# Seven block products on all 16 K tiles for a head's in-projection, chained from raw weight tiles

## The chip, the cores and the metric

One core of one Trainium2 chip. The metric is the device time of one execution of the whole program in microseconds (us); lower is better. The program is one launch with all weights in device memory.

## The reference

Two residual layers on one sequence of T = 512 tokens with D = 2048 channels, all in float32. The first is a gated differential attention layer, the second an RWKV-7 layer. Cut to what the change touches:

```python
def diff_attention_mixer(h, ...):            # h: (1, 512, 2048), RMS-normed x
    proj = h @ w_in                          # 2048 x 8192: q, k, v, gate
    q, k, v, gate = jnp.split(proj, 4, axis=-1)
    q = apply_rope(rms_norm(q.reshape(B, T, 8, 2, 128), q_gain), cos, sin)
    k = apply_rope(rms_norm(k.reshape(B, T, 8, 2, 128), k_gain), cos, sin)
    v = v.reshape(B, T, 8, 256)
    o = causal_diff_attention(q, k, v, lam)  # softmax(q0 k0) - lam softmax(q1 k1), times v
    o = rms_norm(o, subln_w) * (1.0 - lambda_init)
    return (o.reshape(B, T, 2048) * jax.nn.silu(gate)) @ w_out
```

## The kernel before, in words

**Products in three passes.** A float32 product is made of three TensorE matmuls on halves of reduced width: high times high, low times high, high times low. The normed input stands in SBUF, transposed, as 16 pairs hH, hL (128 channels by 512 tokens). Weights come in as raw tiles of 2 K tiles by 512 columns (512 KB) and are split: ACT writes the high half (wh, L105), DVE the low half (wl = raw - wh, L106); wh and wl have two buffers each. A raw tile comes from device memory by `load_w` on SP's queue (buffers wraw, three of them, or the tiles Ta, Tb, Tc), and `add_w` adds a second tile of weights to it in place, by an accumulating DMA on POOL's queue.

**Heads.** The in-projection runs head by head. A head has 512 query and key columns (called c1) and 512 value and gate columns (c2). Head 0 is done in the classical way by `unit_tok`. Heads 1 to 7 go through `unit_head`, which halves tokens (0 to 255, 256 to 511), K tiles and columns, and computes the four output blocks by the seven products of Strassen and Winograd instead of eight. The sums of input blocks that these need (S1, S2, S4 and, in place, S3) are made once, at the end of head 0, by `input_sums`; the sums of weights are made by `add_w`. In this kernel only the first 12 K tiles (two halves of NH4 = 6) go by seven products; the last 4 K tiles, called plain, are multiplied in the classical way, at the start of the head for c1 and at its end for c2.

A product is a loop over groups of KG = 2 K tiles: per group one split and 12 matmuls of 128x512 (two token tiles, two K tiles, three passes); a plain group has 24. The seven products of a head share accumulators: a product is either copied from PSUM (`copy_out`, on ACT) or added to what was copied before (`take`, L528, on DVE). Query and key tiles are named t1, value and gate tiles G and acc1.

The order before, for each head: the plain groups of c1; the upper K half of c1 onto tokens 0 to 255; S1 on the tiles Ta, Tb, Tc (which `first_sums` loaded and added during the head before); the lower K half of c1; S4 on new c2 tiles; S2 on Ta, Tb, Tc after an add; the square product (upper half, tokens 256 to 511) on them after another add; S3 on the S4 tiles after an add; the plain groups of c2.

**Work beside it.** `head_qk` squares, rotates (L269 to L273, on DVE) and normalizes two of a head's four query and key tiles and `turn_qk` turns them (L295, L298, L299); `head_vg` scales values and gates (L315 to L320). The attention of head h - 1 runs as a chain of small steps inside head h: a step is issued at a tick, and `tick` is called once for each matmul of 128x512; a delay before the first step and a gap between two are counted in these ticks.

**Order.** A scheduler places the instructions on each engine from the program's order and from priorities: `high_priority(offset=...)` moves `take` and `head_qk` ahead, `issue_after` keeps an instruction behind another. On an engine, instructions then run strictly in that order.

**Memory.** The pools are const, hp (16 pairs), wraw (3), wh and wl (2 each), small (3) and work. The scratch for the descriptors of POOL's DMAs has its default size.

**The second layer** uses the same splits for its in-projection, two heads of 64 at a time; there, a small triangular system goes through device memory (td from Tm, TT from td, L1344 to L1366).

Of the kernel before, what the change touches and what calls it, by code (L numbers as in the profile page):

```python
# [13 lines left out]
F32 = mybir.dt.float32  # L14
# [43 lines left out]
def rsqrt(g, out, v, n, tag):  # L58

    nc = g.nc  # L60
    m = 1 if tag in ("r4", "r16") else 3
# [125 lines left out]
def rope_tables(g, aps):  # L187
    nc = g.nc
    c = g.lc
    wide = g.work.tile([P, 4, NT, 64], F32, name="rope", tag="Tc", bufs=1)  # L190
    ang, n, sn, cs = [wide[:, i] for i in range(4)]
    rows = g.work.tile([P, 4, P], F32, name="ropein", tag="a", bufs=1)
    pos_i = g.small.tile([P, NT], I32, name="pos_i", tag="posi", bufs=1)
    nc.gpsimd.dma_start(out=pos_i[:], in_=aps["positions"].rearrange("o (t p) -> (o p) t", p=P),)
    pos = g.small.tile([P, NT], F32, name="pos", tag="pos", bufs=1)
# [31 lines left out]
def lambda_full(g, aps):  # L227
    nc = g.nc
    e = []
    both = g.work.tile([P, 4, P], F32, name="lam", tag="at", bufs=1)  # L230
    for i in (1, 2):
        a, b = both[:, 2 * i - 2], both[:, 2 * i - 1]
        nc.gpsimd.dma_start(out=a[:], in_=aps[f"da_lam_q{i}"][0].partition_broadcast(P))
        nc.gpsimd.dma_start(out=b[:], in_=aps[f"da_lam_k{i}"][0].partition_broadcast(P))
        nc.vector.tensor_mul(a[:], a[:], b[:])
        s = g.small.tile([P, 1], F32, name=f"ls{i}", tag=f"ls{i}", bufs=1)
# [15 lines left out]
def head_qk(g, t1s, sq, ts):  # L252
# [5 lines left out]
    for i, t in enumerate(ts):  # L258
        squares = w.tile([P, 512], F32, name="squares", tag=("p0", "p1")[t % 2], bufs=1)
# [9 lines left out]
        nc.vector.tensor_mul(t2v[:, :, :, 0:64], t1v[:, :, :, 64:128], tab(g.S, 0, 64))  # L269
        nc.vector.tensor_mul(t2v[:, :, :, 64:128], t1v[:, :, :, 0:64], tab(g.S, 64, 128))  # L270
        nc.vector.reduce_sum(ss[:, i, :], squares[:].rearrange("p (c d) -> p c d", c=4), AX.X)
        nc.vector.tensor_mul(t1v, t1v, tab(g.C, 0, P))
        nc.vector.tensor_add(t1[:], t1[:], t2[:])  # L273
# [35 lines left out]
def head_vg(g, h, vg, G):  # L309
# [4 lines left out]
    for t in range(NT):  # L314
        nc.scalar.activation(V[:, t, :], vg[t][:, 0:256], AF.Copy, scale=g.rstd0[:, t : t + 1])  # L315
        th = w.tile([P, 256], F32, name="th", tag="th", bufs=1)
# [9 lines left out]
def attention(g, h, qkT, qkL, sq, V, VL, G, gap, rows=None, keys=()):  # L326
# [6 lines left out]
    def scores(t):  # L333
# [5 lines left out]
        for c in range(2):  # L339
# [8 lines left out]
            p_ = w.tile([P, 512], F32, name=f"p{c}", tag=f"p{c}", bufs=1)  # L348
# [7 lines left out]
        b.a = w.tile([P, 512], F32, name="a", tag="a", bufs=1)  # L356
# [106 lines left out]
NH4 = 6  # L463
# [3 lines left out]
def input_sums(g, pairs, late):  # L467
# [3 lines left out]
    if not late:  # L471
        def parts(*tags):

            out, tags = [], list(tags)
            while tags:
# [3 lines left out]
                else:  # L479
                    at = w.tile([P, 2, 2 if t[-1] == "2" else 4, 256], F32R, name=t, tag=t, bufs=1)  # L480
# [44 lines left out]
def take(g, acc, ps, op=ALU.add):  # L525
    with g.tc.high_priority(offset=SCAN):
        for a, p in zip(acc, ps):
            g.nc.vector.tensor_tensor(out=a, in0=a, in1=p[:], op=op)  # L528


def unit_head(g, aps, h, t1s, sq, turned):
# [7 lines left out]
    N, plain = NH4 // KG, range(2 * NH4, KT, KG)  # L539
# [18 lines left out]
    def products(out, lhs, wt, start=False, end=False):  # L558
        first = start
        for t in range(2):  # L560
            for lo in range(2):
# [6 lines left out]
            first = start  # L568

    X, y = pair(), pair()  # L570
    for k0 in plain:
        wt = split(load(k0, c1))
        products(X, block(k0, 256), wt, k0 == plain[0], k0 == plain[-1])
        products(y, block(k0, 0), wt, k0 == plain[0])
    copy_out(g, q[2:], X)
    for i in range(N):
        products(y, block(NH4 + i * KG, 0), split(load(NH4 + i * KG, c1)), end=i == N - 1)
    copy_out(g, q[:2], y)
    X = pair()
    for i in range(N):  # L580
        products(X, form("S1", i), split(g.Ts[i]), i == 0)
        add_w(g, g.Ts[i], c2, NH4 + i * KG)
    copy_out(g, acc[2:], X)
    y = pair()
    for i in range(N):
        products(y, block(i * KG, 0), split(load(i * KG, c1)), i == 0)
    take(g, q[:2], y)
    head_qk(g, t1s, sq, [0, 1])
    b22 = []
    for i in range(N):  # L590
        b22.append(load(NH4 + i * KG, c2))
        products(X, form("S4", i), split(b22[i]), end=i == N - 1)
        add_w(g, b22[i], c2, i * KG)
    G, acc[:2] = gates(g)
    copy_out(g, acc[:2], X)
    for i in range(N):
        products(y, form("S2", i), split(g.Ts[i]))
        add_w(g, g.Ts[i], c1, NH4 + i * KG)
    take(g, acc[:2], y, ALU.subtract)
    X = pair()  # L600
    for i in range(N):
        products(X, block(NH4 + i * KG, 256), split(g.Ts[i]), i == 0, i == N - 1)
    take(g, q[2:], X)
    for i in range(N):
        products(y, form("S3", i), split(b22[i]), end=i == N - 1)
    take(g, acc[2:], y, ALU.subtract)
    take(g, q[2:], y)
# [12 lines left out]
    if h < NH - 1:  # L620
        first_sums(g, aps, h + 1)
    take(g, acc[:2], y)
    take(g, acc[2:], X)
    return acc, G
# [156 lines left out]
def layer0(g, aps):  # L781
# [3 lines left out]
    with ExitStack() as cx:  # L785
# [4 lines left out]
                 for tag in ("V", "VL", "acc1", "G", "Ta", "Tb")]  # L790
        rest_x = g.work.tile([P, KT - 2 * NH4, T], F32, name="xT", tag="qkT", bufs=1)
        xT = [p[:, i] for i in range(2) for p in pairs] + [rest_x[:, k] for k in range(KT - 2 * NH4)]
# [52 lines left out]
        for cb, tags in enumerate((("qkL",), ("sA2", "sB2"), ("qkT",), ("qkL",))):  # L845
# [18 lines left out]
        g.mask = g.lc.tile([P, T], F32, name="mask")  # L864
# [13 lines left out]
        for h in range(NH):  # L878
            if h:
                Chain(g, attention(g, h - 1, *before, 28 if h > 1 else 26, keys=rest), 20)  # L880
# [11 lines left out]
            if h:  # L892
                vg, G = unit_head(g, aps, h, t1s, sq, lambda: Chain(g, keys(2), 6))
            else:
# [4 lines left out]
                first_sums(g, aps, 1)  # L899
# [8 lines left out]
            before = qkT + (sq,) + head_vg(g, h, vg, G)  # L908
# [25 lines left out]
        def store_x(cb, t):  # L934
            xr = xs[cb][:, t, :]
            junk = g.work.tile([P, 512], F32, name="junkx", tag="a", bufs=1)
            with tc.high_priority(offset=SCAN if cb > 1 else 0):
# [7 lines left out]
                 {"S1": one("p0", "p1"), "S2": one("sA2"), "S4": one("acc1"), "S3": one("Ta")},  # L945
# [24 lines left out]
        def banks(i):  # L970
            if i < 2:
# [4 lines left out]
        load = loader(g, aps["da_w_out"], ((g.wraw, "wraw", 3), (g.work, "V", 1), (g.wraw, "wraw", 3),  # L976
                                              (g.work, "G", 1), (g.wraw, "wraw", 3)))

        rs = g.work.tile([P, NT], F32, name="rs1", tag="rs1", bufs=1)
        ss = g.work.tile([P, NT], F32, name="ss1", tag="ss1", bufs=1)  # L980
# [217 lines left out]
def stage1(g, j, k, up):  # L1198
# [19 lines left out]
    p.gam = g.small.tile([P, NC_], F32, name="gam", tag="gam")  # L1218
# [318 lines left out]
def layer1(g, aps):  # L1537
    nc, tc = g.nc, g.tc
    with ExitStack() as cx:
# [127 lines left out]
        def banks(i):  # L1667
            if i == 0:
# [4 lines left out]
        load = loader(g, aps["rw_w_out"], ((g.wraw, "wraw", 3), (w, "G1", 2), (g.wraw, "wraw", 3), (w, "LT", 1),  # L1673
                                              (g.wraw, "wraw", 3), (w, "G1", 2)))
# [4 lines left out]
def body(ctx, tc, nc, aps):  # L1679
# [63 lines left out]
```

## Time and profile before

| | us |
|---|---|
| runs | 2139.86, 2146.2, 2145.77 |
| median of the runs | 2145.77 |
| span of the profiled execution | 2147.2 |
| head 1 / heads 2 to 6 / head 7 | 94.8 / 91.3 to 91.8 / 92.8 |
| second layer, 935 to 2050 us | 1115.0 |

The span is the time from the first to the last instruction in the profiled execution; it is 1.4 us over the median of the runs. A head is measured between the last gate operations (L320) of two heads. In the views, names are those of the tiles in the program, `L106` is a line of the kernel, PE is TensorE, PEld its weight loads, DVE is VectorE, ACT is ScalarE, POOL is GpSimd, SP is SyncE. The time of a single PE row is a pipelined latency, so PE's pace is read from start to start.

### The profile page before, as it was taken

The numbers are of one execution on the slowest core, as the hardware profiler recorded it, in microseconds if no ns is written. First come the engines' busy times: TensorE is split into PE (matmuls) and PEld (weight loads), VectorE is DVE, ScalarE is ACT, GpSimd is POOL, SyncE is SP. The second block draws the span as 40 slices with busy tenths as digits, with TensorE's granted clock in tenths as the row PEclk, the third lists the DMA queues.
The fourth block names the chain that finished last, engine by engine and source line by source line (L and its number), as shares of the span: only waits on it lengthen the run. The fifth ranks groups of instructions, "written<-read, shape, count | busy, mean of one in ns | idle before, by whom it ended". The sixth has DMA issues, their size and how long they took to land.

```text
span 2147.2 us, 34137 instructions
## 1 busy us (share of the span) xinstructions
PE 2112.4 (98%) x11936; PEld 1718.6 (80%) x11936; DVE 1606.9 (75%) x4130; ACT 1129.2 (53%) x2251; POOL 361.1 (17%) x723
## 2 busy tenths in 40 slices
PE   9999999999999999999999999999999999999999
PEld 7788888888888888878677788888888888778887
DVE  6877888878788876576768678877777788767645
ACT  5755555656555544355555555565545555545322
POOL 1010101101011100101222212222222122221001
PEclk9999999999999999999999999999999999999999
DMA  7566767677686946622222222323333232336555
GB/s 242 180 153 180 179 160 191 153 182 177 157 196 167 296 143 173 154 81 94 79 69 87 86 81 91 91 84 94 94 94 94 84 91 91 108 117 192 178 163 120
DMA packets 142541, 292.51 MB, mean 136 GB/s; under 512 B 47920, under 2 KB 65328, under 8 KB 142368
## 3 DMA queue, kind: packets, MB, share of 16 engines
q1 hardware_dynamic: 78528, 191.13, 27.0%
q0 software_dynamic: 21184, 73.06, 18.1%
q10 hardware_dynamic: 42656, 26.14, 4.0%
q8 instruction: 94, 1.54, 0.3%
q14 instruction: 79, 0.65, 0.1%
HBM read 266.61 MB, written 23.66 MB: 135 GB/s over the span
## 4 chain that ended last, share of the span: by engine, by line
PE 35%; DVE 9%; DMA 3%; issue 2%; ACT 1%; POOL 0%; SPq 0%; ACTq 0%; DVEq 0%; POOLq 0%
PE pp L122 22%; PE pt L122 5%; DMA td<-Tm 2%; DVE tmpl L1340 2%; DVE wl L106 2%; DVE Tm L1342 1%; PE gp L1275 1%; PE sm L1453 1%; DMA TT<-td 1%; PE sm L1464 1%; PE sm L1471 1%; PE px L1372 1%; PE px L1382 1%; DVE VS L1475 1%; PE pt L1195 0%
## 5 line engine op out<-in xcount | busy, mean ns | idle before, releaser
L106 DVE TENSOR_TENSOR wl<-wraw,wh 128x1024 fp32r<-128x1024 f32 (+2 forms) x305 | 373.3, 1224 | 225.6 <-ACT wh L105 223.8
L105 ACT CAST wh<-wraw 128x1024 fp32r<-128x1024 f32 (+2 forms) x305 | 318.4, 1044 | 354.5 <-PE pp L122 174.2
L122 PE MATMUL pp<-hH,wl 128*128 128x512 f32 x1024 | 416.4, 407 | 0.0
L122 PE MATMUL pp<-hL,wh 128*128 128x512 f32 x1024 | 415.2, 405 | 0.0
L122 PE MATMUL pp<-hH,wh 128*128 128x512 f32 x1024 | 413.0, 403 | 0.0
L122 PEld LDWEIGHTS pp<-hH,wh 128*128 128x128 f32 x1024 | 194.9, 190 | 36.1 <-issue 2.3
L122 PEld LDWEIGHTS pp<-hL,wh 128*128 128x128 f32 x1024 | 194.7, 190 | 35.3 <-issue 0.2
L122 PEld LDWEIGHTS pp<-hH,wl 128*128 128x128 f32 x1024 | 194.7, 190 | 33.0 <-DVE wl L106 0.4
L564 PE MATMUL pp<-wh,hH 128*128 128x512 f32 x560 | 220.9, 394 | 0.0
L564 PE MATMUL pp<-wh,hL 128*128 128x512 f32 x560 | 219.0, 391 | 0.0
L564 PE MATMUL pp<-wl,hH 128*128 128x512 f32 x560 | 175.0, 394 | 0.1
L122 PE MATMUL pp<-wh,hH 128*128 128x512 f32 x372 | 146.3, 395 | 3.0 <-ACT hH L1076 3.0
L122 PE MATMUL pp<-wl,hH 128*128 128x512 f32 x372 | 146.9, 395 | 0.6 <-DVE wl L106 0.6
L122 PE MATMUL pp<-wh,hL 128*128 128x512 f32 x372 | 146.3, 393 | 0.0
L1340 DVE SCALAR_TENSOR_TENSOR tmpl<-LT,Tm 128x60 f32<-128x60 f32 (+24 forms) x496 | 134.6, 271 | 11.6
L1459 POOL COPY SA<-VS 64x64 f32<-64x64 f32 x224 | 62.7, 280 | 431.4 <-DVE VS L1475 347.6
L564 PEld LDWEIGHTS pp<-wh,hL 128*128 128x128 f32 x560 | 105.2, 188 | 21.5
L564 PEld LDWEIGHTS pp<-wh,hH 128*128 128x128 f32 x560 | 105.2, 188 | 21.4 <-ACT wh L105 0.3
L564 PEld LDWEIGHTS pp<-wl,hH 128*128 128x128 f32 x560 | 103.2, 188 | 21.7 <-DVE wl L106 0.8
L1342 DVE TENSOR_TENSOR Tm<-Tm,tmpl 128x60 f32<-128x60 f32 (+24 forms) x496 | 103.3, 208 | 10.5
L1456 ACT COPY rhs<-sm 64x64 f32<-64x64 f32 x256 | 52.6, 206 | 66.7 <-PE sm L1453 64.0
L122 PEld LDWEIGHTS pp<-wh,hH 128*128 128x128 f32 x372 | 70.4, 189 | 17.8 <-ACT hH L1076 3.7
(388 smaller groups left out, 4252.6 us busy)
## 6 DMA issues: line engine op xcount, KB each, us to landing
wraw<-in_rw_w_in_dram SPq DMA_DIRECT2D x128, 512.0 KB
wraw<-in_da_w_in_dram SPq DMA_DIRECT2D x92, 512.0 KB
wraw<-in_da_w_out_dram SPq DMA_DIRECT2D x26, 512.0 KB
wraw<-in_rw_w_out_dram SPq DMA_DIRECT2D x26, 512.0 KB
Tc<-in_da_w_in_dram POOLq DMA_DIRECT2D x21, 512.0 KB, 6.6
Ta<-in_da_w_in_dram POOLq DMA_DIRECT2D x21, 512.0 KB, 5.4
Tb<-in_da_w_in_dram POOLq DMA_DIRECT2D x21, 512.0 KB, 5.5
wraw<-in_da_w_in_dram POOLq DMA_DIRECT2D x21, 512.0 KB, 5.4
```

What stands on the lines that cost most here:

```text
L105: a = nc.scalar.copy(hi[:, ks], raw[:, ks])
L106: d = nc.vector.tensor_sub(lo[:, ks], raw[:, ks], hi[:, ks].bitcast(F32))
L122: m = nc.tensor.matmul(out, a, b, start=s, stop=e, skip_group_check=skip)
L564: m = nc.tensor.matmul(out[t][:], x, wt[lo][:, k, :], start=first, stop=end and lo == 1 and k == KG - 1, skip_group_check=True)
L1275: m = nc.tensor.matmul(gp[h][:, i * P : (i + 1) * P], BK[r_, c0 + i, :, :], p.AR[r_, c0 + i, :, :], start=True, stop=True)
L1340: nc.vector.scalar_tensor_tensor(tt, LT[:, i : i + 1, i + 1 :].to_broadcast([P, s, n]), n2[:, i : i + 1], Tm[:, 0:s, i : i + 1].to_broadca ...
L1342: nc.vector.tensor_add(Tm[:, 0:s, i + 1 :], Tm[:, 0:s, i + 1 :], tt)
L1372: nc.tensor.matmul(px[hi, c * HALF : (c + 1) * HALF], p.G[lo, c, 0, h, HALF:C], T1[lo, c, :], start=True, stop=True, tile_position=(b0, b0 ...
L1382: nc.tensor.matmul(px[lo, N + c * HALF : N + (c + 1) * HALF], X[hi, c, :], TT[hi, c, h, HALF:C], start=True, stop=True, tile_position=(b0 ...
L1453: nc.tensor.matmul(sm[:, 0:P], both(p.G[:, c, 0]), both(VS[:, c]), start=True, stop=True)
L1456: nc.scalar.copy(rhs[r_, :], sm[r_, h * C : h * C + C])
L1459: nc.gpsimd.tensor_copy(p.SA[r_, c - 1, :], VS[r_, c, h, :])
```

## The change

`NH4` goes from 6 to 8: all 16 K tiles go by seven products, four groups each, and the plain groups are gone. There is a fourth chained tile, Td.

The tiles Ta to Td are loaded raw (c1, lower K half) and used raw for the product that was made from separate loads; then the c2 tiles of the lower half are added for S1, those of the upper half for S2, and the c1 tiles of the upper half for the square product. So a head still moves 28 tiles of 512 KB, of which 16 instead of 12 are accumulated by POOL's queue and 12 instead of 16 loaded by SP's.

The order of a head becomes: upper half of c1 (copied out), lower half of c1 raw, S1, S4, S2, the first two tiles of `head_qk`, the transposes of the keys, S3, `head_vg`, the square product, and then `take` and `head_qk` for the other two query and key tiles. The seventh head has an order of its own: S1, S2, square, S3, `head_qk`, S4. The attention of the head before starts after 56 ticks for heads 2 to 7 where it was 20, with a gap of 26 where it was 28.

The room in SBUF comes from smaller or shared tiles: the descriptor scratch is set to 2048 bytes, the pool small has 2 buffers, the mask is BF16, the second softmax row is written in place in PSUM, several tiles share tags; wraw gets a fourth buffer, in both layers. `input_sums` covers eight pairs instead of six.

```diff
-NH4 = 6
+NH4 = 8
...
-def first_sums(g, aps, h):
-    g.Ts = [g.work.tile([P, KG, 512], F32, name="T" + "abc"[i], tag="T" + "abc"[i], bufs=1) for i in range(NH4 // KG)]
+def first_tiles(g, aps, h):
+    g.Ts = [g.work.tile([P, KG, 512], F32, name="T" + "abcd"[i], tag="T" + "abcd"[i], bufs=1) for i in range(NH4 // KG)]
     for i, t in enumerate(g.Ts):
-        load_w(g, t, vg_cols(aps, h), i * KG, slice(0, KG))
-        add_w(g, t, qk_cols(aps, h), i * KG)
+        load_w(g, t, qk_cols(aps, h), i * KG, slice(0, KG))
...
+    def all_groups(out, lhs, raw, start=False, end=False, then=None):
+        for i in range(N):
+            r = raw(i)
+            products(out, lhs(i), r, start and i == 0, end and i == N - 1)
+            if then:
+                add_w(g, r, then[0], then[1] + i * KG)
...
+    chained = lambda i: g.Ts[i]
+    y = pair()
+    all_groups(y, lambda i: block(NH4 + i * KG, 0), lambda i: load(NH4 + i * KG, c1), True, True)
     copy_out(g, q[:2], y)
+    y = pair()
+    all_groups(y, lambda i: block(i * KG, 0), chained, True, False, (c2, 0))
+    take(g, q[:2], y)
     X = pair()
+    all_groups(X, lambda i: form("S1", i), chained, True, last, (c2, NH4))
     copy_out(g, acc[2:], X)
+    b22 = []
+    if not last:
+        s4(X, b22, end=True)
+        G, acc[:2] = gates(g)
+        copy_out(g, acc[:2], X)
+    all_groups(y, lambda i: form("S2", i), chained, then=(c1, NH4))
...
+    turned()
+    third()
+    copy_out(g, q[2:], y)
+    values = head_vg(g, h, acc, G)
+    X = square()
+    first_tiles(g, aps, h + 1)
     take(g, q[2:], X)
     with g.tc.high_priority(offset=AHEAD):
         head_qk(g, t1s, sq, [2, 3])
-    turned()
-    y, X = pair(), pair()
-    rest = []
-    for k0, t in zip(plain, "ab"):
-        rest.append(g.work.tile([P, KG, 512], F32, name="T" + t, tag="T" + t, bufs=1))
-        load_w(g, rest[-1], c2, k0, slice(0, KG))
-    for k0, raw in zip(plain, rest):
-        wt = split(raw)
-        for out, t0 in ((X, 256), (y, 0)) if k0 == plain[0] else ((y, 0), (X, 256)):
-            products(out, block(k0, t0), wt, k0 == plain[0], k0 == plain[-1])
...
-                Chain(g, attention(g, h - 1, *before, 28 if h > 1 else 26, keys=rest), 20)
+                Chain(g, attention(g, h - 1, *before, 26, keys=rest), 56 if h > 1 else 20)
...
-    g.wraw = ctx.enter_context(tc.tile_pool(name="wrawp", bufs=3))
+    g.wraw = ctx.enter_context(tc.tile_pool(name="wrawp", bufs=4))
...
-    g.small = ctx.enter_context(tc.tile_pool(name="small", bufs=3))
+    g.small = ctx.enter_context(tc.tile_pool(name="small", bufs=2))
...
-    nc = _bacc.Bacc("TRN2", target_bir_lowering=False, num_devices=1)
+    nc = _bacc.Bacc("TRN2", target_bir_lowering=False, num_devices=1, dynamic_dma_scratch_size=2048)
```

More of the change, by code (lines that the diff above doesn't have):

```diff
@@ L258, in head_qk @@
     for i, t in enumerate(ts):
-        squares = w.tile([P, 512], F32, name="squares", tag=("p0", "p1")[t % 2], bufs=1)
+        squares = w.tile([P, 512], F32, name="squares", tag="al", bufs=1)
         t1 = t1s[t]
@@ L538, in unit_head @@
     q = [t[:] for t in t1s]
-    N, plain = NH4 // KG, range(2 * NH4, KT, KG)
+    N = NH4 // KG
+    last = h == NH - 1
     def pair():
@@ L556, in form, with products @@
         return lambda k, t: [x[:, t * P : (t + 1) * P] for x in g.sums[nm][i * KG + k]]
-    def products(out, lhs, wt, start=False, end=False):
-        first = start
+    def products(out, lhs, raw, start=False, end=False):
+        wt = split(raw)
         for t in range(2):
+            first = start
             for lo in range(2):
@@ L567, in products @@
                         first = False
[L568 to L577, printed above, removed]
+    def all_groups(out, lhs, raw, start=False, end=False, then=None):
[4 more added lines that the diff above has]
+                add_w(g, r, then[0], then[1] + i * KG)
@@ L578, in unit_head, with s4, raw @@
+    def s4(out, keep, start=False, end=False):
+        def raw(i):
+            keep.append(load(NH4 + i * KG, c2))
+            return keep[-1]
+        all_groups(out, lambda i: form("S4", i), raw, start, end, None if last else (c2, 0))
+    chained = lambda i: g.Ts[i]
+    y = pair()
+    all_groups(y, lambda i: block(NH4 + i * KG, 0), lambda i: load(NH4 + i * KG, c1), True, True)
     copy_out(g, q[:2], y)
+    y = pair()
+    all_groups(y, lambda i: block(i * KG, 0), chained, True, False, (c2, 0))
@@ L594, in unit_head @@
[L594 to L602, printed above, removed]
+    b22 = []
[4 more added lines that the diff above has]
+    all_groups(y, lambda i: form("S2", i), chained, then=(c1, NH4))
@@ new lines, in unit_head, with square, third @@
+    if last:
+        G, acc[:2] = gates(g)
+    take(g, acc[:2], y, ALU.subtract, acc[2:] if last else None)
+    def square():
+        X = pair()
+        all_groups(X, lambda i: block(NH4 + i * KG, 256), chained, True, True)
+        return X
+    def third():
+        for i in range(N):
+            if last:
+                b22.append(load(NH4 + i * KG, c2))
+                add_w(g, b22[i], c2, i * KG)
+            products(y, form("S3", i), b22[i], end=i == N - 1)
+        take(g, acc[2:], y, ALU.subtract)
@@ L603, in unit_head @@
+    head_qk(g, t1s, sq, [0, 1])
+    if last:
+        copy_out(g, q[2:], square())
+        third()
+        take(g, q[2:], y)
+        with g.tc.high_priority(offset=AHEAD):
+            head_qk(g, t1s, sq, [2, 3])
+        turned()
+        X = pair()
+        s4(X, [], True, True)
+        take(g, acc[:2], X)
+        return head_vg(g, h, acc, G)
+    turned()
+    third()
+    copy_out(g, q[2:], y)
+    values = head_vg(g, h, acc, G)
+    X = square()
+    first_tiles(g, aps, h + 1)
     take(g, q[2:], X)
-    for i in range(N):
-        products(y, form("S3", i), split(b22[i]), end=i == N - 1)
@@ L620, in unit_head @@
[L620 to L624, printed above, removed]
+    return values
 class Rows:
@@ L789, in layer0 @@
         pairs = [g.work.tile([P, 2, T], F32, name="pair", tag=tag, bufs=1)
-                 for tag in ("V", "VL", "acc1", "G", "Ta", "Tb")]
-        rest_x = g.work.tile([P, KT - 2 * NH4, T], F32, name="xT", tag="qkT", bufs=1)
-        xT = [p[:, i] for i in range(2) for p in pairs] + [rest_x[:, k] for k in range(KT - 2 * NH4)]
+                 for tag in ("V", "VL", "acc1", "G", "Ta", "Tb", "Tc", "Td")]
+        xT = [p[:, i] for i in range(2) for p in pairs]
         ss = g.const.tile([P, NT], F32, name="ss0")
@@ L863, in layer0 @@
         nc.vector.tensor_scalar(g.hrstd0[:], g.rstd0[:], 0.5, None, ALU.mult)
-        g.mask = g.lc.tile([P, T], F32, name="mask")
+        g.mask = g.lc.tile([P, T], BF16, name="mask")
         nc.gpsimd.memset(g.mask[:], 0.0)
@@ L975, in layer0 @@
         T2 = g.work.tile([P, KG, 512], F32, name="T2", tag="Tb", bufs=1)
[L976 to L980, printed above, removed]
+        load = loader(g, aps["da_w_out"], ((g.wraw, "wraw", 4), (g.work, "V", 1), (g.wraw, "wraw", 4),
+                                              (g.work, "G", 1), (g.wraw, "wraw", 4)))
+        rs = g.small.tile([P, NT], F32, name="rs1", tag="ss")
+        ss = g.small.tile([P, NT], F32, name="ss1", tag="rr")
         def scale(cb, t):
```

55 lines of the change are left out of this document (21 added, 34 removed).

## The prediction, made before the changed kernel ran

> **What bounds the kernel now.** I read the page first, then the windows by stage, then the groups of the engine that sets the pace, then timelines of the places that the change touches, and last the DMA issues.
>
> From the page, the span and each engine's busy time with its share:
>
> ```profile
> span 2147.2 us, 34137 instructions
> PE 2112.4 (98%) x11936; PEld 1718.6 (80%) x11936; DVE 1606.9 (75%) x4130; ACT 1129.2 (53%) x2251; POOL 361.1 (17%) x723
> ```
>
> The windows, cut where the last gate product of each head (L320) ends: head 1, head 3, head 7, and most of the second layer. Columns: length, then busy time (and count) of PE, PEld, DVE, ACT, POOL, then granted clock, DMA share, GB/s.
>
> ```profile
> core 0: us, PE busy (x) PEld busy (x) DVE busy (x) ACT busy (x) POOL busy (x), PEclk, DMA share, GB/s
> 102.40:197.20 94.80, 94.72 (x451) 78.19 (x452) 76.11 (x201) 54.07 (x97) 10.14 (x12) 1.00 0.66 158
> 288.50:379.80 91.30, 91.30 (x438) 75.67 (x437) 76.24 (x205) 51.58 (x93) 10.18 (x12) 1.00 0.71 173
> 654.40:747.20 92.80, 91.45 (x437) 75.47 (x436) 76.38 (x205) 51.57 (x93) 12.01 (x17) 1.00 0.83 239
> 935.00:2050.00 1115.00, 1094.12 (x7186) 881.04 (x7185) 820.40 (x2164) 598.47 (x1313) 254.83 (x585) 0.99 0.33 100
> ```
>
> A head takes 91.3 us and PE has no gap in it, at a granted clock of 1.00; DVE is busy for 76.2 us of it. PE bounds these stages, so fewer matmuls is the right currency, provided that DVE stays hidden group by group and not only on average. The start of a product group on PE, one row per matmul, in head 2 (start, length, what):
>
> ```profile
> 302.03 0.39 PE L564 MATMUL pp<-wh,hH 128*128 128x512 f32 x1
> 302.26 0.39 PE L564 MATMUL pp<-wh,hL 128*128 128x512 f32 x1
> 302.49 0.62 PE L564 MATMUL pp<-wl,hH 128*128 128x512 f32 x2
> 302.94 0.39 PE L564 MATMUL pp<-wh,hH 128*128 128x512 f32 x1
> ```
>
> The 0.39 us is a latency. What a matmul costs is the step from start to start: (302.94 - 302.03) / 4 = 0.2275 us. A group of 12 thus lasts 2.73 us.
>
> **The gain.** Before, a head has 12 K tiles in seven products, 7 x 3 x 12 = 252 matmuls, and 4 K tiles plain, 2 x 48 = 96: 348. After it has 7 x 4 x 12 = 336. That is 12 less in each of 7 heads: 84 x 0.2275 = **19.1 us** of PE, where PE has no gaps. Nothing else leaves PE: the order of the compiled programs differs by 84 matmuls and by nothing else in count.
>
> **What DVE and ACT get.** Splits (one L105 on ACT, one L106 on DVE) rise from 25 to 28 a head, takes (L528) fall from 98 to 58 in all. Groups of DVE, with count, busy, mean ns, and idle time with its releaser:
>
> ```profile
> L106 DVE TENSOR_TENSOR wl<-wraw,wh 128x1024 fp32r<-128x1024 f32 x299 | 368.1, 1231 | 224.4 <-ACT wh L105 222.5
> L528 DVE TENSOR_TENSOR t<-t,pp 128x512 f32<-128x512 f32 x42 | 28.1, 680 | 2.4 <-PE pp L564 2.4
> L492 DVE SCALAR_TENSOR_TENSOR hL<-pair,norms,hH 128x256 fp32r<-128x256 f32 x6 | 2.8, 475 | 0.0
> L343 DVE CUSTOM_DVE_ANT_0 sc<-sc,mask 128x512 f32<-128x512 f32 x16 | 11.1, 694 | 0.7
> L1366 DVE STREAM_TRANSPOSE T<-TT 64x256 f32<-64x256 f32 x32 | 14.1, 439 | 18.5 <-DMA TT<-td 18.1
> ```
>
> Three more splits by some 1.14 us from start to start make 3.4 us, 40/7 takes fewer by 0.60 us make 3.4 us: DVE stays at about 76 us, now of 88.6 (91.3 - 2.73), or 86%. On average it hides. The question is where it comes in lumps. The largest lump of before, in head 3:
>
> ```profile
> 363.00 1.22 DVE L106 TENSOR_TENSOR wl<-Ta,wh 128x1024 fp32r<-128x1024 f32 x1 [1.49 <-ACT wh L105]
> 364.14 0.68 DVE L528 TENSOR_TENSOR acc<-acc,pp 128x512 f32<-128x512 f32 x1
> 364.74 0.68 DVE L528 TENSOR_TENSOR t<-t,pp 128x512 f32<-128x512 f32 x1
> ...
> 366.53 0.41 DVE L269 TENSOR_TENSOR t<-t,ropeS 128x256 f32<-128x256 f32 x1
> 366.87 0.41 DVE L270 TENSOR_TENSOR t<-t,ropeS 128x256 f32<-128x256 f32 x1
> 367.20 0.68 DVE L271 TENSOR_REDUCE ss<-squares 128x4 f32<-128x512 f32 x1
> 367.80 0.68 DVE L272 TENSOR_TENSOR t<-t,ropeC 128x512 f32<-128x512 f32 x1
> ...
> 371.46 0.16 DVE L274 TENSOR_SCALAR ss<-ss 128x8 f32<-128x8 f32 x1
> 371.53 1.22 DVE L106 TENSOR_TENSOR wl<-Tb,wh 128x1024 fp32r<-128x1024 f32 x1
> 373.11 0.86 PE L564 MATMUL pp<-wl,hH 128*128 128x512 f32 x3
> ```
>
> These rows give the prices: a split 1.14 us to the next start, an operation of 512 elements 0.60, of 256 elements 0.33, a tiny one 0.08. Between the two splits lie 8.5 us, takes and the rotation of the last two query and key tiles (head_qk). It is hidden only because it lies beside the plain groups, which have 24 matmuls, 5.46 us each: wl is written at 372.75, PE reads it at 373.11, 0.36 us of room.
>
> **(a) The same lump after the change.** There are no plain groups. The rotation now follows the square product, the last of its head, and by the order of DVE's instructions it stands between the low halves of the first and the second group of the next head, groups of 2.73 us. Let S be the start of the next head's first group. DVE begins the lump at S - 0.9. In it lie 2 takes (1.20), 4 operations of L269/L270 (1.34), 5 of L271 to L273 (3.00), a tiny one and the split (1.22 to its end): 6.8 us, plus about 0.4 us in which the second take awaits the last matmul. The second wl is written at about S + 6.2. PE's order puts the 8 matmuls on wh of that group first, so wl is wanted at S + 2.73 + 8 x 0.2275 = S + 4.55. PE stands still for some **1.65 us** (1.2 to 2.4), at the six heads 2 to 7: 9.9 us. The third split is done 1.8 us after the second, when it is wanted, so nothing follows on.
>
> **(b) The middle of a head.** Takes of second and subtracted products, the gates' copies and the shifted attention (it starts 56 ticks after the head's start where it waited 20) fall among splits. Adding the same prices in the order of DVE's instructions, one or two groups have 4.3 to 5.4 us of DVE against 2.73 to 3.2 us of PE, and the room that stands before them (some 1.5 us, at most 3) takes most of it. I take 0.4 us a head, 2.4 us for six; bounds 0 and 2.5 us a head.
>
> **(c) The start of head 1.** input_sums makes 8 pairs instead of 6, and its last 8 low halves (L492, 0.39 us from start to start) with a 0.60 us L299 stand between the splits of the first two groups: about 6 us with the split, against 2.73 us. I take 2.0 us, bounds 1 and 4.
>
> **(d) Head 7** has its own order: the same rotation, with key transposes' L299, stands between the first groups of the last product. Room as in (a), a lump of 8.5 us as in before: 2.9 us, bounds 1.5 and 4.
>
> **DMA.** Issues with KB each and median us to landing:
>
> ```profile
> Tc<-in_da_w_in_dram POOLq DMA_DIRECT2D x21, 512.0 KB, 6.6
> Ta<-in_da_w_in_dram POOLq DMA_DIRECT2D x21, 512.0 KB, 5.4
> wraw<-in_da_w_in_dram POOLq DMA_DIRECT2D x21, 512.0 KB, 5.4
> LT<-ltd POOLq DMA_DIRECT2D x64, 132.0 KB, 2.8
> td<-Tm POOLq DMA_DIRECT2D x16, 128.0 KB, 3.0
> ```
>
> A head still moves 28 tiles, but 16 instead of 12 are adds issued by POOL, 28 more in all. A chained tile comes back four groups later: with the attention between, 4 x 3.16 us (88.6 / 28) less the 2.1 us that its split needs ahead, 10.5 us against 5.4 to 6.6. It is hidden, by 4 us; if landing took 10.5 us or more, each late tile would cost its excess. POOL is busy 10.2 us of a head, so the longer queue there costs nothing. In head 7 SP's queue has loads of the next stage's rows ahead of the last product's weights; by the order they wait only for the square product, which ends a whole product earlier: nothing.
>
> [...]
>
> **The rest.** The descriptor scratch falls from its default to 2048 bytes; no row shows its price. It can be nothing; or POOL waits for room in a fuller ring. In the second layer that would tell: PE's chain there waits for td to come back (18.1 us of idle before L1366, row above), so each us more on td's 3.0 costs about 16. The nearest row is td's own; were it to double, 48 us; I take 0, since the adds of a head are some 3 us apart and those of the second layer further, and keep 8 us (0.5 each) in the range. The split of the second layer's up-weights stands some 20 instructions earlier on DVE: 0, bounds -3 and +3. The mask in BF16, the exp written in place, the fourth weight buffer: each stands on engines with 15 us or more of idle in a head, 0, bounds -1 and +2.
>
> **Sum.** -19.1 + 9.9 + 2.4 + 2.0 + 2.9 = -1.9, against the profiled 2147.2 us: 2145.3. The profile's span lies 1.4 us above the median of the runs, so I forecast **2144 us**. A difference under 0.3%, 6.4 us, is about what a measurement of this kernel can't tell from none.
>
> **Rivals.**
>
> 1. *The gain arrives.* The lumps overlap more than I add up: takes start before the square is done, or the rotation sinks behind the splits. For it: DVE has 12 us a head left, and the lump in before fits with 0.36 us to spare, so the sum is sensitive to single instructions. Against: the order on DVE is fixed in the program and PE can't go around a missing wl. With half of (a) to (d) gone, 2135; with nearly all, 2128. Chance 0.29.
>
> 2. *DVE becomes the bound of a head's middle* (slower). If the groups of (b) have no room left in front of them, because each stall is followed by the next, the price is the upper bound: 2.1 us more in six heads, 12.6, so 2157; with the upper end of (a), 4.5 more, 2161. It decides as soon as the room at S2 and S3 is below 0.5 us where before has 1.5. Chance 0.20.
>
> 3. *The small descriptor ring holds up POOL*, in the second layer 16 times 0.5 to 1 us: 2152 to 2160. Against it: in most of the trace POOL's transfers stand alone. Chance 0.08.
>
> 4. *Chained tiles come late*, the adds landing in over 10.5 us beside SP's loads; 2 us at one tile a head, 14 us: 2158. The DMA share of 0.71 speaks for it, 4 us of room against it. Chance 0.06.
>
> **How the numbers follow.** My forecast, 2138 to 2150, has 0.37. Its own parts: 0.25 within 0.3% (2139.3 to 2152.2), 0.07 faster, 0.05 slower. Rival 1 gives 0.27 faster, 0.02 same; rival 2 0.02 same, 0.18 slower; rivals 3 and 4 together 0.05 same, 0.09 slower. That makes 0.34 faster, 0.34 same, 0.32 slower. The forecast alone would reach from 2138 to 2150; the range takes in most of rivals 1 and 2: 2129 to 2160.
>
> **What would show it.** Right: heads 2 to 6 take about 90.6 us (91.3 - 2.73 + 1.65 + 0.4), PE waits for wl (L106) once early in each head, about 1.65 us, and the wait ends with a wl on a weight tile that follows head_qk; 84 matmuls fewer at L565; POOL's adds land in under 8 us; the second layer keeps its 1115 us within 3. The gain has arrived if a head takes 88.6 us. Wrong: PE waiting for ACT's wh or for a DMA in the heads, waits of over 1 us at two or more places of a head, or a second layer longer by over 5 us.

## The result and the profile after

| | median of the runs, us | ratio to the kernel before | 95% interval |
|---|---|---|---|
| before | 2144.79 (5 runs, 2139.86 to 2146.2) | | |
| after | 2160.25 (5 runs, 2154.87 to 2171.03) | 1.0081 | 1.0055 to 1.0107 |

The change makes the kernel 0.8% slower. The forecast was 2144 with a range to 2160; the result lies just beyond it. The profiled execution of the changed kernel is the slowest of the five, 2171.03 us with a span of 2169.3. Among the runs further down, one of the six executions of e6 took 5270.77 us at a full granted clock; why isn't known, and it is left out of that row's ratio and means, not of its median.

The page of after, span and busy times:

```profile
span 2169.3 us, 34050 instructions
PE 2110.7 (97%) x11852; PEld 1711.5 (79%) x11852; DVE 1614.6 (74%) x4129; ACT 1149.3 (53%) x2278; POOL 386.2 (18%) x751
```

The 84 matmuls are gone (11936 to 11852), the span is 22.1 us longer. Where it went, by windows that are cut at the first matmul of head 1, the last of head 7, and the first px of the first and of the last of 16 pairs of heads in the second layer. px (L1372 before, L1385 after) are the small products that use what came back through td. Columns as in the prediction's windows. Before:

```profile
103.20:744.10 640.90, 639.49 (x3049) 528.84 (x3048) 530.06 (x1409) 360.89 (x652) 73.08 (x89) 1.00 0.72 180
744.10:1041.10 297.00, 290.57 (x1422) 237.20 (x1420) 201.18 (x422) 134.53 (x230) 27.39 (x51) 1.00 0.46 133
1041.10:1956.60 915.50, 898.61 (x6111) 722.14 (x6111) 692.77 (x1925) 504.03 (x1145) 232.13 (x530) 0.99 0.31 93
```

After, with heads 3 and 7 by themselves:

```profile
103.00:748.60 645.60, 627.58 (x2966) 512.02 (x2966) 539.67 (x1402) 378.89 (x673) 99.95 (x120) 1.00 0.82 188
748.60:1045.70 297.10, 289.41 (x1423) 237.28 (x1421) 198.63 (x414) 135.01 (x232) 27.66 (x51) 1.00 0.47 130
1045.70:1978.80 933.10, 911.65 (x6110) 733.28 (x6110) 689.53 (x1925) 504.45 (x1145) 232.78 (x529) 0.97 0.31 91
283.60:374.70 91.10, 89.20 (x425) 72.76 (x424) 76.89 (x200) 54.09 (x97) 13.60 (x16) 1.00 0.79 173
648.90:748.60 99.70, 91.55 (x426) 74.08 (x425) 81.73 (x214) 51.89 (x91) 18.21 (x24) 0.98 0.94 253
```

The seven heads, which lost 84 matmuls, take 4.7 us more: the first six 2.3 us less, head 7 6.9 us more. The stage between is equal. The pairs of the second layer, whose instructions on PE are the same in number and order, take 17.6 us more in this execution, at a granted clock of 0.97 instead of 0.99. There PE is idle for 4.6 us more (21.5 for 16.9) and busy for 13.0 us more with the same work. So there are two losses, one expected and one not.

**The heads.** PE's first gap of head 2, with what DVE does meanwhile:

```profile
196.65 0.39 PE L565 MATMUL pp<-wh,hL 128*128 128x512 f32 x1
198.60 0.97 PE L565 MATMUL pp<-wl,hH 128*128 128x512 f32 x3 [1.56 <-DVE wl L106]
...
196.65 0.68 DVE L272 TENSOR_TENSOR t<-t,ropeC 128x512 f32<-128x512 f32 x1
197.25 0.16 DVE L274 TENSOR_SCALAR ss<-ss 128x8 f32<-128x8 f32 x1
197.32 1.22 DVE L106 TENSOR_TENSOR wl<-wraw,wh 128x1024 fp32r<-128x1024 f32 x1
```

From start to start that is 1.95 us where a matmul needs 0.23: 1.72 us, once in each of heads 2 to 7. Two gaps are larger, at the end of head 0 and in head 7:

```profile
102.27 0.76 PE L295 MATMUL pt<-ident,t 128*128 128x128 f32 x2 [3.36 <-ACT t L280]
...
703.07 1.12 PE L363 MATMUL pt<-ident,a 128*128 128x128 f32 x4 [2.15 <-DVE yTl L400]
```

**The second layer.** PE's wait ahead of px, summed over the kernel (busy, mean ns, then the idle time and its releasers), before and after:

```profile
L1372 PE MATMUL px<-T,G 32*32 32x32 f32 x512 | 21.8, 194 | 13.8 <-DVE T L1366 10.4 <-DVE y L1396 3.3
```

```profile
L1385 PE MATMUL px<-T,G 32*32 32x32 f32 x512 | 23.2, 199 | 19.8 <-DVE T L1379 14.9 <-DVE y L1409 4.9
```

Six us more. Five and a half of them stand in three pairs, the first (4.9 us of wait for 3.3), the third (3.2 for 1.3) and the fifteenth (2.6 for 0.6); most others wait some 0.2 us longer. What comes late is the start of td's DMA on POOL. The last operation on Tm (DVE) and the DMA (POOL) in one undisturbed pair, that is one without half clock, before:

```profile
1452.75 0.41 DVE L1343 TENSOR_TENSOR Tm<-Tm,LT 128x256 f32<-128x256 f32 x1
...
1453.46 1.00 POOL L1344 DMA_DIRECT2D td<-Tm  x1 [2.81 <-DVE s L1509]
```

and after:

```profile
1465.12 0.41 DVE L1356 TENSOR_TENSOR Tm<-Tm,LT 128x256 f32<-128x256 f32 x1
...
1466.09 1.00 POOL L1357 DMA_DIRECT2D td<-Tm  x1 [3.07 <-DVE s L1521]
```

0.30 us after Tm's end before, 0.56 us after, in 14 and in 13 of the 16 pairs. The landing is the same (3.0 us in both). The longer wait ahead of the first px isn't the late start's doing alone: in e1, where td starts as late, it is 3.5 us.

Most of the 17.6 us is clock. In the traces of before and after the clock is either 1.0 or 0.5; half clock comes in 5 and in 10 stretches of one to four times 3.41 us, and in each trace their starts lie on one grid of that step, within 3 ns. Windows of that length around one px of after (length, PE busy, granted clock, DMA share, GB/s):

```profile
1651.80:1655.20 3.40, 3.27 (x15) 1.00 0.33 55
1655.20:1658.60 3.40, 2.19 (x44) 1.00 0.60 175
1658.60:1662.00 3.40, 3.40 (x49) 0.51 0.03 8
1662.00:1665.50 3.50, 3.50 (x19) 0.51 0.06 9
1665.50:1668.90 3.40, 3.40 (x18) 1.00 0.01 1
```

The window with the gap is followed by two at half clock, and this pair takes 64.4 us where an undisturbed one takes 61.4. At half clock a matmul of 512 columns takes 0.43 us from start to start (L565 at 103.62, 104.04 and 104.47 us of after), at full clock 0.23. Over the profiled execution half clock adds up to 30.7 us before and 68.3 us after: half of the difference, 18.8 us, is about the loss.

Since every run comes with its mean granted clock, each can be split: span x (1 - clock) is **lost to half clock**, span x clock is its **full-clock time**. The second hardly varies between runs of one kernel (a standard deviation of 1 to 3 us), the first does (2 to 7 us). In the means: before 2130 to 2133 full-clock and 12 to 13 lost (80 runs in four groups), after 2136.2 and 22.9 (5 runs). So of some 15 us about 10 are half clock, and 5 are what the waits, in the heads and ahead of px, cost beyond the 19.1 us of matmuls that are gone.

### The profile page after: what moved, and what is told of

Read it like the earlier page. It is cut to its first block, busy times and chain, and to the rows that moved or that the text cites. A ratio compares the mean times of both kernels' runs of the same rounds, so it can differ in the third digit from the quotient of the medians.

```text
span 2169.3 us, 34050 instructions
## 1 busy us (share of the span) xinstructions
PE 2110.7 (97%) x11852; PEld 1711.5 (79%) x11852; DVE 1614.6 (74%) x4129; ACT 1149.3 (53%) x2278; POOL 386.2 (18%) x751
## 4 chain that ended last, share of the span: by engine, by line
PE 49%; DVE 14%; DMA 5%; issue 3%; ACT 2%; POOL 0%; SPq 0%; ACTq 0%; POOLq 0%; DVEq 0%
PE pp L122 29%; PE pt L122 5%; PE pp L565 3%; DVE wl L106 3%; DVE tmpl L1353 2%; DMA td<-Tm 2%; DVE Tm L1355 2%; PE gp L1288 2%; DMA TT<-td 1%; PE sm L1466 1%; PE sm L1477 1%; PE px L1395 1%; PE lora L122 1%; PE px L1385 1%; ACT wh L105 1%
## 5 line engine op out<-in xcount | busy, mean ns | idle before, releaser
L106 DVE TENSOR_TENSOR wl<-wraw,wh 128x1024 fp32r<-128x1024 f32 (+2 forms) x291 | 356.1, 1224 | 230.5 <-ACT wh L105 222.3
L105 ACT CAST wh<-wraw 128x1024 fp32r<-128x1024 f32 (+2 forms) x291 | 303.5, 1043 | 328.1 <-PE pp L122 153.5
L565 PE MATMUL pp<-wh,hH 128*128 128x512 f32 x448 | 176.7, 394 | 0.1
L565 PE MATMUL pp<-wh,hL 128*128 128x512 f32 x448 | 175.8, 392 | 0.0
L565 PE MATMUL pp<-wl,hH 128*128 128x512 f32 x448 | 142.2, 397 | 9.4 <-DVE wl L106 9.4
L122 PE MATMUL pp<-wh,hH 128*128 128x512 f32 x372 | 145.8, 392 | 0.9 <-ACT hH L1089 0.9
L122 PE MATMUL pp<-wl,hH 128*128 128x512 f32 x372 | 146.0, 393 | 0.4 <-DVE wl L106 0.4
L122 PE MATMUL pp<-wh,hL 128*128 128x512 f32 x372 | 145.6, 391 | 0.1
L1355 DVE TENSOR_TENSOR Tm<-Tm,tmpl 128x60 f32<-128x60 f32 (+24 forms) x496 | 104.0, 210 | 10.6
L565 PEld LDWEIGHTS pp<-wl,hH 128*128 128x128 f32 x448 | 82.5, 189 | 27.8 <-DVE wl L106 11.9
L565 PEld LDWEIGHTS pp<-wh,hH 128*128 128x128 f32 x448 | 84.6, 189 | 17.7 <-issue 0.5
L565 PEld LDWEIGHTS pp<-wh,hL 128*128 128x128 f32 x448 | 84.5, 189 | 17.3
L1479 ACT COPY VS<-sm 64x64 f32<-64x64 f32 x256 | 52.7, 206 | 59.5 <-PE sm L1477 54.0
```

What stands on the lines that cost most here:

```text
L105: a = nc.scalar.copy(hi[:, ks], raw[:, ks])
L106: d = nc.vector.tensor_sub(lo[:, ks], raw[:, ks], hi[:, ks].bitcast(F32))
L122: m = nc.tensor.matmul(out, a, b, start=s, stop=e, skip_group_check=skip)
L565: m = nc.tensor.matmul(out[t][:], x, wt[lo][:, k, :], start=first, stop=end and lo == 1 and k == KG - 1, skip_group_check=True)
L1355: nc.vector.tensor_add(Tm[:, 0:s, i + 1 :], Tm[:, 0:s, i + 1 :], tt)
L1479: nc.scalar.copy(VS[r_, c, h, :], sm[r_, P : P + C])
```

## Experiments

Each row has 6 or 12 runs. Ratios are to the kernel before on the same chip, with 95% intervals; e1 to e4, e5 to e8, e9 and e10, e11 and e12 each ran on one chip, so across these groups the ratios compare better than the medians.

| run | median, us | ratio | full-clock time | lost to half clock |
|---|---|---|---|---|
| e1_before_ring2048 | 2160.59 | 1.0065 (1.0045 to 1.0086) | 2132.6 | 27.0 |
| e2_before_wraw4 | 2147.84 | 1.0014 (0.9999 to 1.0029) | 2131.9 | 14.9 |
| e11_before_wraw4_ring8192 | 2140.32 | 0.9973 (0.9956 to 0.9989) | 2131.4 | 7.8 |
| e6_before_td_sp | 2134.13 | 0.9936 (0.9915 to 0.9958) | 2127.9 | 4.7 |
| e7_before_ring_td_sp | 2134.22 | 0.9931 (0.9911 to 0.9952) | 2126.6 | 5.0 |
| e5_after_td_sp | 2144.15 | 0.9988 (0.9973 to 1.0003) | 2129.6 | 12.5 |
| e3_after_rot_free | 2152.81 | 1.0029 (1.0012 to 1.0046) | 2127.7 | 23.7 |
| e4_after_rot_free_7 | 2155.71 | 1.0040 (1.0024 to 1.0056) | 2126.3 | 27.5 |
| e8_after_free_td_sp | 2132.61 | 0.9925 (0.9902 to 0.9948) | 2118.7 | 11.7 |
| e9_free_td_sp_delay40 | 2129.23 | 0.9926 (0.9912 to 0.9940) | 2117.6 | 10.6 |
| e10_free_td_sp_delay20 | 2126.02 | 0.9919 (0.9901 to 0.9937) | 2113.8 | 12.0 |
| e12_after_free_delay20 | 2149.29 | 1.0002 (0.9985 to 1.0019) | 2121.0 | 25.4 |

**The ring alone** (e1), that is the smaller scratch for POOL's descriptors, in the kernel before:

```diff
-    nc = _bacc.Bacc("TRN2", target_bir_lowering=False, num_devices=1)
+    nc = _bacc.Bacc("TRN2", target_bir_lowering=False, num_devices=1, dynamic_dma_scratch_size=2048)
```

> The kernel before with one edit: the descriptor scratch of POOL's DMAs is 2048 bytes. All orders stay. Theory (small ring): in the changed kernel the issue of td on POOL starts 0.56 us after the end of the last operation on Tm (L1356) where before it starts 0.30 us after it (L1343). If the ring does that, it does it here too: 0.5 to 0.6 us, PE's wait ahead of px grows by about 0.25 us in each of 16 pairs (13.8 us in all to some 18), more of the 3.4 us windows at half clock follow it, and the time rises by 4 to 15 us. Rival (order of the second layer, or chance): the issue stays at 0.30 us and the time within 3 us of before.

Its timeline, and its wait ahead of px:

```profile
1462.29 0.42 DVE L1343 TENSOR_TENSOR Tm<-Tm,LT 128x256 f32<-128x256 f32 x1
...
1463.26 1.01 POOL L1344 DMA_DIRECT2D td<-Tm  x1 [3.07 <-DVE s L1508]
```

```profile
L1372 PE MATMUL px<-T,G 32*32 32x32 f32 x512 | 22.8, 198 | 16.4 <-DVE T L1366 12.9 <-DVE y L1396 3.5
```

0.55 us from Tm to td, 2.6 us more wait, and 15.5 us of time, of which 2 us are full-clock time and the rest half clock. One line of the change, which moves no instruction on DVE or POOL, costs in this kernel as much as the whole.

**The ring and the fourth weight buffer** (e2), again in the kernel before:

```diff
+    ... dynamic_dma_scratch_size=2048)
-    g.wraw = ctx.enter_context(tc.tile_pool(name="wrawp", bufs=3))
+    g.wraw = ctx.enter_context(tc.tile_pool(name="wrawp", bufs=4))
```

with the loaders of both output projections at 4.

> The kernel before with the scratch of 2048 bytes and a fourth wraw buffer in both layers, so that the second layer's DVE order becomes that of the changed kernel, while the first layer keeps six-tile halves and plain groups. Theory (small ring): as the run with the ring alone, within 3 us. Rival (order of the second layer): the split of the up-weights that is moved ahead delays td and px, the run with the ring alone is as fast as before and this one is 4 to 15 us slower.

Both theories missed. td starts as late as in e1 and the wait ahead of px is 15.9 us, yet only 14.9 us are lost to half clock. So the same late td goes with 27.0 us lost in e1 and with 14.9 in e2, where the orders around it are others. Which of the moved instructions helps isn't settled.

**The same with a larger ring** (e11): the scratch at 8192 bytes, all orders as in e2.

> The kernel before with a fourth wraw buffer in both layers, as in the run with a scratch of 2048 bytes (2147.8 us), and with the same orders on every engine, but a scratch of 8192 bytes. Theory (a ring that is short of room costs td 0.26 us): the issue of td is back at 0.30 us after Tm, the wait ahead of px falls from 15.9 to 13 to 14 us in all, the time to 2139 to 2145. Rival (a ring of any size but the default costs the 0.26 us): the issue stays at 0.56 us and the time at 2148 within 3 us.

As the theory has it: 7.5 us faster than with 2048. td starts 0.30 us after Tm again in ten pairs; in the other six it starts 0.34 to 0.46 us later than that. Whether this ring runs short there isn't shown, since with the default scratch two pairs start late as well, by 0.75 us. The wait ahead of px is 13.6 us.

**td on SP's queue** (e5 in the kernel after, e6 before, e7 before with the small ring):

```diff
-    nc.gpsimd.dma_start(out=g.td[j % 2].rearrange("q l t -> l q t"), in_=Tm[:])
+    nc.sync.dma_start(out=g.td[j % 2].rearrange("q l t -> l q t"), in_=Tm[:])
```

> The changed kernel with one edit: td goes out on SP's queue, right ahead of the TT loads that wait for it, and not on POOL's. No descriptor of it passes the small ring. Theory (the changed kernel loses in the second layer because td's issue is 0.26 us later and PE's wait ahead of px falls into windows of low use that are followed by half clock): the wait ahead of px falls from 0.65 us to under 0.3 us in the undisturbed pairs, the time lost to half clock, span x (1 - clock), falls from 22.9 us to 8 to 15 us, and the run takes 2140 to 2152 us instead of 2160. Rival (half clock comes from elsewhere, and the longer wait only goes with it): lost time stays at 20 us or more, the time above 2154.

> The kernel before with td on SP's queue, scratch at its default. Theory: PE's wait ahead of px falls from 0.45 us to near nothing, and the 13.3 us that the kernel before loses to half clock fall below 10; time 2135 to 2142. Rival: as before, 2145 within 3 us.

> The kernel before with the scratch of 2048 bytes and td on SP's queue; its orders are those of the run before it in this list. Theory (the small ring costs through td alone): within 3 us of that run, far below the 2160.6 us of the small ring with td on POOL. Rival (the ring costs through the other DMAs of POOL as well, the loads of LT above all): 8 us or more above it.

The wait ahead of px in e5:

```profile
L1385 PE MATMUL px<-T,G 32*32 32x32 f32 x512 | 21.9, 196 | 8.5 <-DVE T L1379 4.9 <-DVE y L1409 3.4
```

19.8 to 8.5 us, the time from 2160 to 2144, both as expected. In e7 the small ring costs nothing any more (2134.22 against 2134.13): it costs through td alone. And the kernel before gains 0.6% as well. The move also shifts some DVE instructions in the second layer, which these runs don't separate from it.

These runs also bound what the ring explains. With td on SP's queue in both, on one chip, the changed kernel is still 10 us slower than the one before (2144.15 against 2134.13), 1.7 us of it full-clock time and 7.8 half clock. So in the changed kernel the ring isn't the whole loss. A part of the half clock is known: in all eight traces with the changed heads a window of it follows the end of head 0, and in none of the six with the old heads. The rest is open.

**The rotation without its priority** (e3 in heads 1 to 6, e4 in head 7 too):

```diff
     take(g, q[2:], X)
-    with g.tc.high_priority(offset=AHEAD):
-        head_qk(g, t1s, sq, [2, 3])
+    head_qk(g, t1s, sq, [2, 3])
```

> The changed kernel without the raised priority of the last rotation (head_qk of tiles 2 and 3) in heads 1 to 6: its operations then lie between the splits of the next head's first four groups, instead of all between the first and the second. Theory (the lump costs the heads their gain): the six gaps of 1.56 us in PE at the start of heads 2 to 7 vanish, a head takes 89.3 to 89.6 us instead of 91.2, the stage of the heads is about 10 us shorter, and the time falls by 8 to 12 us. Rival (DVE has no room, the wait comes back at the next groups): a head stays above 90.5 us.

> As the run before it in this list, and in head 7 too the rotation has no raised priority, so that the gap of 2.69 us ahead of the second group of the last product goes. Theory: head 7 is 2.5 to 3 us shorter than with the other edit alone, the rest equal; the gap of 2.15 us in head 7 behind a store of ys and the half-clock window next to it stay. Rival: the turned keys and with them the last attention come later, and the output projection that waits for it gives the 3 us back.

DVE in e3 at the start of head 2: the split comes between the operations of the rotation.

```profile
194.39 1.22 DVE L106 TENSOR_TENSOR wl<-wraw,wh 128x1024 fp32r<-128x1024 f32 x1
195.52 0.42 DVE L270 TENSOR_TENSOR t<-t,ropeS 128x256 f32<-128x256 f32 x1
195.86 0.68 DVE L271 TENSOR_REDUCE ss<-squares 128x4 f32<-128x512 f32 x1
196.45 0.68 DVE L272 TENSOR_TENSOR t<-t,ropeC 128x512 f32<-128x512 f32 x1
197.07 1.23 DVE L106 TENSOR_TENSOR wl<-wraw,wh 128x1024 fp32r<-128x1024 f32 x1
```

The six gaps of 1.56 us are gone, and a head takes 89.9 us, not 89.3 to 89.6: a wait of 0.8 us ahead of the key transposes (L295) has come up in their place, so that a part of the expectation missed. The full-clock time falls by 8.5 us. In e4 the gap of 2.69 us goes too: head 7 is 4.1 us shorter in the trace (96.2 to 92.1), 1.7 us of it a half-clock window that e3 has there, and the stage behind it 0.7 us longer. The runs are no faster than those of e3 all the same, with 1.4 us less full-clock time and 3.8 us more lost to half clock, a difference that 12 runs each hardly carry.

**Both repairs** (e8), and then the start of the attention (e9: 40 ticks, e10: 20 as before):

```diff
-                Chain(g, attention(g, h - 1, *before, 26, keys=rest), 56 if h > 1 else 20)
+                Chain(g, attention(g, h - 1, *before, 26, keys=rest), 20 if h > 1 else 20)
```

> The changed kernel with both rotations free of their raised priority and td on SP's queue. Theory: the full-clock time of the same kernel with td on POOL, 2126.3 us, less up to 6 us of waits ahead of px, plus 10 to 15 us lost to half clock: 2132 to 2141 us, faster than the kernel before (2145) and, within 2 us, than that with td on SP or beside it. Rival: the half-clock windows stay, 2150 or more.

> The kernel with both rotations free and td on SP's queue, and the attention of the head before starting after 40 ticks instead of 56. Theory (the prediction's part b: the shifted attention puts softmax and key transposes on DVE where S2 and S3 want their splits): the gap of 0.8 us ahead of the key transposes (L295) in each of heads 2 to 7 goes, a head takes 88.8 to 89.3 us instead of 90.0, the full-clock time falls by 4 to 7 us from 2118.7, the time to 2124 to 2130. Rival (the gap is set by the turned keys and not by the attention): heads stay at 90.0 and the time within 3 us of 2132.6.

> As the run before it in this list, with the 20 ticks of the kernel before. Theory: the attention then ends ahead of the products S2 and S3 by as much or more; the heads as with 40 ticks, within 0.4 us a head, with some more waits near S4, where the softmax of the fourth block now falls. Rival: heads of 90.0 us, no better than with 56.

e8 comes out in time as expected, 2132.61 us; its full-clock time, 2118.7, is 1.6 us below what the theory allows. With 40 ticks the gap ahead of L295 stays at 0.80 us, since ACT now has the first block's exponentials (L349) in front of the scaling (L280) that the transposes wait for: the theory missed there. With 20 ticks it is 0.27 us. The heads of e10, all seven and head 3:

```profile
104.90:731.10 626.20, 622.59 (x2966) 511.89 (x2966) 533.81 (x1390) 380.43 (x673) 99.92 (x120) 1.00 0.84 192
284.00:372.90 88.90, 88.63 (x425) 72.92 (x424) 76.47 (x200) 54.41 (x97) 13.60 (x16) 1.00 0.80 178
```

88.9 us a head against 91.3 before: 2.4 of the 2.73 us arrive. e10 has the shortest time, 2126.02 us. Against the kernel before with the same td (e6) its full-clock time is 14 us lower and its loss to half clock 7 us higher. Whether it is the faster of the two isn't settled: the medians, from two chips, differ by 8 us, but the intervals of the ratios (0.9919 and 0.9936) overlap.

**e10 with td back on POOL** (e12):

> The changed kernel with both rotations free and the attention starting after 20 ticks, but td on POOL's queue as in the change. Theory (two losses that add: one of the heads and one through td): heads of 88.9 us, full-clock time 2120 to 2123 us, 20 to 28 us lost to half clock, so 2142 to 2150 us, no faster than before; 16 to 24 us behind the same kernel with td on SP's queue (2126.0). Rival (half clock depends on the heads' timing): within 8 us of 2126.

Heads of 89.0 us, 2121.0 us full-clock, 25.4 lost: 23 us slower than e10. The two losses add, as expected, and without the second repair the first brings only a tie with before.

## Why the prediction was wrong, step by step

In the profiled execution the seven heads, for which the sum has -1.9 us, took 4.7 us more, and the pairs of the second layer, for which it has 0, took 17.6 us more. A second layer longer by over 5 us was one of the prediction's own signs of being wrong.

**The gain**: right. 84 matmuls less, and in e10 2.4 us a head.

**(a)**: right, 1.72 us at six heads for 1.65, at the place that was named, and removed by taking the rotation apart.

**(b)**: half right. The two small gaps are 0.34 us a head for 0.4. But PE's stream of product matmuls also stretched by some 0.6 us a head without a gap to see (89.20 us busy in head 3, where 91.3 less 2.73 is 88.57), so that head 3 takes 91.1 where 90.6 was forecast and 91.3 stood before. In e10 the stretch is gone (88.63); its cause is open.

**(c)**: within its bounds (1 to 4), wrong place and a price left out. Head 1 itself has under 0.1 us of gaps; at the end of head 0 PE waits 3.36 us, where it waited 0.56 before, and then runs 3.4 us at half clock. In the trace operations of input_sums stand there on DVE between the rotation's last steps; no run takes them away.

**(d)**: the gap was 2.69 for 2.9 us. Missed in head 7 was DVE behind a store of ys: POOL's adds and loads of the next stage's rows run during S3, the DMA share is 0.94 in this head, L400 waits 2.13 us for its buffer, PE 2.15 us, with a half-clock window behind it. The cause of the slow store, the loads, was only read from the DMA share, and the traces of e3 and e4 don't have this wait. Head 7 takes 99.7 us where the sum gives 95.0 (92.8 - 2.73 + 1.65 + 0.4 + 2.9).

**The descriptor ring**: this is the step that failed. It was priced by td's landing, taken at 0, and kept in the range with 8 us. Landing did stay at 3.0 us; the issue became 0.26 us later. In the kernel before, the ring alone costs 15.5 us (e1), 2.2 us of it full-clock time and 13.7 us half clock, and with td off POOL's queue nothing (e7). Beside the order of e2 it costs some 8 us (e2 against e11, where a larger ring takes its place). Rival 3 named the place and the time, 2152 to 2160, with a chance of 0.08, which was too low for an edit without a single row to price it. That its time comes so near is partly luck: it had POOL held up by 0.5 to 1 us sixteen times, not by 0.26 us with half clock behind it. And the ring isn't all: with td on SP's queue the change still loses 10 us (e5 against e6), most of it to half clock.

**The clock**: not in the sum at all, the second step that failed. The windows showed 1.00 in the heads and 0.99 in the second layer, and I read the 0.99 as nothing, though 1% of 1115 us is 11 us. In the trace of after only two windows of 3.41 us, at 99 and at 1041 us, have no start of a matmul (PE's waits of 3.36 us and, ahead of the first px, 4.92 us). Behind them lie three of the 20 windows at half clock, 68.3 us, of this execution; the other 17, in eight stretches, follow windows that matmuls fill to a share of 0.16 to 0.48, counted as in the last section.

**The DMA**: right. POOL's adds land as fast as before, and td too:

```profile
wraw<-in_da_w_in_dram POOLq DMA_DIRECT2D x28, 512.0 KB, 5.8
Ta<-in_da_w_in_dram POOLq DMA_DIRECT2D x21, 512.0 KB, 5.6
...
td<-Tm POOLq DMA_DIRECT2D x16, 128.0 KB, 3.0
```

The added adds cost PE nothing that a gap shows.

Rival 1 (the gain arrives) is what the heads of e10 make of the change. Rival 2 didn't come: the middle of a head had room. Nor did rival 4: the adds land in 5.5 to 6.0 us.

## What to carry to other kernels

An edit that only frees memory deserves a row of its own: look for who waits on the resource that it shrinks, and measure it alone. When a step that runs dozens of times waits on a short chain, price not only the wait but the half clock that can come with it (13.7 of the 15.5 us in e1), and split each run into full-clock time and lost time before comparing: between runs of one kernel the first had a standard deviation of 1 to 3 us here, the second of 2 to 7. Where work is removed from the bounding engine, look for the longest unbroken run of the second engine, and break it up.

## What the runs showed of the hardware

What share of a window do PE's matmuls fill where half clock follows? I cut the 14 traces of this case into the 3.41 us grid on which the clock changes, and took for each window at full clock the share that its matmuls fill (columns x 0.2275 us / 512, each from its start). Windows whose clock isn't on record, in the first microseconds, and the last one of each trace are left out. All 44 windows below 0.35 were followed by half clock, 19 of 63 between 0.35 and 0.50, and none of 8510 above 0.50. This is what was seen to go together; no run varies the share by itself. In before and after alone it is 7 of 7, 8 of 16 and none of 1203. A gap of 0.61 us ahead of a px of after, among small matmuls in a window with a share of 0.47, was followed by half clock; a gap of 1.56 us among matmuls of 512 columns was not in any of 12 cases of after and e5. An undisturbed pair of the second layer takes 61.4 us, which is 18.0 such windows: in after the first px of four pairs in a row, from 1409.9 to 1594.3 us, comes 0.46 to 0.52 us after the start of a window. Whether that has to do with the lost time, which varies between runs of one kernel, no run here tests.
